# Seven half-block products in place of eight in the last product of a hybrid layer, and the recurrence's output in a score bank

## The chip, the cores and the metric

The kernel runs on one core of one Trainium2 chip. The metric is the device time of an execution in microseconds, the median of several runs. The engines are named as in the profile: PE is TensorE (PEld its weight loads), DVE is VectorE, ACT is ScalarE, POOL is GpSimd, SP is SyncE. Matmuls accumulate in PSUM, in eight banks of 128 x 512 float32; everything else lives in SBUF.

## The reference

One decoder layer on 512 tokens and 1024 channels. A combined input projection feeds a block-sparse attention branch (8 heads of 64) and a gated linear recurrence (4 heads of 128). Both branches are projected up to 1024 channels, gated and merged; then comes what this case is about:

```
h = x + merged @ w_out                                  # 1024 x 1024
ple = (p @ w_ple) * sigmoid(h @ w_ple_gate)             # 256 x 1024 and 1024 x 1024
out = h + ple
```

## The kernel before, in words

Activations lie with channels on the partitions and the 512 tokens along the free axis, so a block of 128 channels is one tile of 128 x 512. A float32 operand a is split into a high half (a copy on ACT in the reduced format fp32r, names ending in h) and a low half (the difference, on DVE, names ending in l). Each product of 128 x 128 weights is then three matmuls: high x high, low x high, high x low (`mm3`, L288).

After the branches come three stages, each over eight output blocks n of 128 channels:

- the merge (ua, L1032), which leaves mh and ml, eight blocks of each;
- the output product (h, L1042 to L1055): eight input blocks by three matmuls of 512 tokens, 24 in all, then `hf = h + x` on DVE (L1049) and its split into hh and hl;
- the last stage (L1067 to L1095): the small product pe of two input blocks (6 matmuls, p @ w_ple), the last product g of eight input blocks (24 matmuls, h @ w_ple_gate), the sigmoid on ACT (L1092), a multiplication by pe and an addition of hf on DVE (L1093, L1094), and the store. The last block is cut into two halves of 256 tokens, so that less is left to do after the last matmul.

Weight blocks of w_out and w_ple_gate (512 KB, tiles wf64 to wf79) are loaded by POOL's queue (L261) into four buffers, and split by `w_split` (L271 on ACT, L272 on DVE) two blocks ahead of use (LD, L41); loads run three further ahead (LATE, L43).

The order of PE's instructions is the order in which the code is written, with side work (attention, recurrence) let in by a clock of nominal times (`tick`, L130). A scheduler places the instructions of ACT, DVE, POOL and SP; `held` and `behind` pin one behind another, `high_priority` draws work forward. PSUM is given out from three pools: "mm" (3 banks, most products), "g" (2) and "a" (3, the attention's scores, and pe). A product that gets a bank waits until the last reader of what was in it is done.

The recurrence's output products (hop, L681 to L690) take a bank of "mm". At the program's start eight matmuls on constants (WARM, L47, L188) keep PE busy until the first operands are there.

## Time and profile before

| | us |
|---|---|
| median of 3 runs (458.33 to 459.59) | 458.77 |
| the profiled execution's own time | 456.21 |
| its span, first to last instruction | 454.4 |
| PE busy in the span | 448.5 |
| the output product h, from 352.39 | 43.52 |
| the last stage, 395.91 to the end | 58.5 |

The profile's durations are those of one execution, 2.6 us below the median; sums are made against its span. A row of the chain of waits in order of time has start, duration, engine, tile and line. A row of the groups has line, engine, operation, tiles and shapes, count, busy time, mean ns of one, and the idle time before it with what ended that. Matmul rows overlap: one lasts 0.389 us with 512 tokens, and the next starts 0.227 us later.

### The profile page before, as it was taken

How to read it: one execution, taken by the hardware profiler on the slowest of the kernel's cores; microseconds unless marked ns; L12 is line 12 of the kernel's file. 1: busy time of each engine (PE TensorE's matmuls, PEld its weight loads, DVE VectorE, ACT ScalarE, POOL GpSimd, SP SyncE). 2: the span in 40 equal slices, each digit the busy share in tenths (PEclk: the TensorE clock that was granted, in tenths of full speed). 3: DMA queues.
4: the chain of work that ended last, by engine and by line, in shares of the span. 5: the costliest groups of instructions: out<-in, count | busy, mean ns of one | idle time of the engine just before them, and what ended most of it. 6: DMA issues, size and time to landing. Idle time of an engine off the chain costs nothing.

```text
span 454.4 us, 8097 instructions
## 1 busy us (share of the span) xinstructions
PE 448.5 (99%) x3064; PEld 373.0 (82%) x3064; DVE 303.0 (67%) x616; ACT 275.4 (61%) x532; POOL 38.6 (8%) x77
## 2 busy tenths in 40 slices
PE   9999999999999999999999999999999999999996
PEld 8888888888888888878788888878888888888886
DVE  5869593886898787858995864654569744544322
ACT  5958574737689696879987894884335433222201
POOL 1000100000000000010101000101220100000000
PEclk9999999999999999999999999999999999999999
DMA  8802323167592446162526243365631644230111
GB/s 257 320 1 93 140 101 119 57 226 184 184 249 71 129 134 172 44 197 67 175 83 190 67 133 124 108 196 152 234 100 47 230 141 140 92 115 25 46 48 46
DMA packets 31846, 59.49 MB, mean 131 GB/s; under 512 B 6976, under 2 KB 16960, under 8 KB 31808
## 3 DMA queue, kind: packets, MB, share of 16 engines
q0 software_dynamic: 9056, 32.51, 21.5%
q1 hardware_dynamic: 22608, 26.47, 19.7%
q8 instruction: 24, 0.39, 0.4%
q14 instruction: 14, 0.11, 0.1%
q10 hardware_dynamic: 144, 0.01, 0.0%
HBM read 48.74 MB, written 4.98 MB: 118 GB/s over the span
## 4 chain that ended last, share of the span: by engine, by line
PE 86%; ACT 5%; DVE 4%; SPq 2%; DMA 1%; issue 1%; DVEq 0%
PE ga L288 10%; PE g L288 10%; PE h L288 10%; PE gb L288 5%; PE ub L288 5%; PE aq L418 5%; PE ak L418 5%; PE ua L288 5%; PE av L418 5%; PE bi L418 4%; PE bf L288 4%; PE bg L288 4%; PE ag L288 4%; PE pe L288 2%; PE bq L288 2%; SPq L859 2%
## 5 line engine op out<-in xcount | busy, mean ns | idle before, releaser
L271 ACT ACTIVATE wh<-wf 128x1024 fp32r<-128x1024 f32 (+1 forms) x78 | 75.5, 968 | 91.6 <-issue 32.2
L272 DVE TENSOR_TENSOR wl<-wf,wh 128x1024 fp32r<-128x1024 f32 (+1 forms) x78 | 86.5, 1109 | 49.5 <-ACT wh L271 49.2
L261 POOL DMA_DIRECT2D wf<-in_w_tr_dram x30 | 15.9, 530 | 171.6 <-DVE wl L272 133.7
L843 ACT ACTIVATE pb<-pb,ps 128x128 f32<-128x128 f32 (+3 forms) x32 | 17.7, 553 | 20.0 <-DVE ps L841 19.9
L288 PE MATMUL g<-hh,wh 128*128 128x512 f32 (+1 forms) x72 | 26.3, 365 | 0.0
L288 PE MATMUL g<-hl,wh 128*128 128x512 f32 (+1 forms) x72 | 26.3, 365 | 0.0
L288 PE MATMUL g<-hh,wl 128*128 128x512 f32 (+1 forms) x72 | 26.3, 365 | 0.0
L288 PE MATMUL gb<-xh,wh 128*128 128x512 f32 x64 | 25.1, 392 | 0.7 <-ACT hu L514 0.7
L288 PE MATMUL ga<-xh,wh 128*128 128x512 f32 x64 | 25.2, 394 | 0.0
L288 PE MATMUL gb<-xl,wh 128*128 128x512 f32 x64 | 24.9, 390 | 0.0
L288 PE MATMUL ga<-xh,wl 128*128 128x512 f32 x64 | 24.9, 389 | 0.0
L288 PE MATMUL ga<-xl,wh 128*128 128x512 f32 x64 | 24.9, 389 | 0.0
L288 PE MATMUL gb<-xh,wl 128*128 128x512 f32 x64 | 24.9, 389 | 0.0
L288 PE MATMUL h<-mh,wh 128*128 128x512 f32 x64 | 24.9, 389 | 0.0
L288 PE MATMUL h<-ml,wh 128*128 128x512 f32 x64 | 24.9, 389 | 0.0
L288 PE MATMUL h<-mh,wl 128*128 128x512 f32 x64 | 24.9, 389 | 0.0
L841 DVE CUSTOM_DVE_ANT_0 pb<-s,bias 128x128 f32<-128x128 f32 (+3 forms) x28 | 12.9, 491 | 6.6 <-DMA bias<-in_ed_dram 3.3
L1049 DVE TENSOR_TENSOR hf<-h,xres 128x512 f32<-128x512 f32 x8 | 5.5, 691 | 16.5 <-PE h L288 16.5
L845 ACT ACTIVATE pb<-pb,ps 128x128 f32<-128x128 f32 (+3 forms) x32 | 16.0, 550 | 0.0
L542 ACT ACTIVATE hx<-hx 128x512 f32<-128x512 f32 x24 | 14.8, 623 | 1.4 <-DVE hx L541 1.3
L288 PEld LDWEIGHTS g<-hh,wl 128*128 128x128 f32 x72 | 13.6, 189 | 2.2
L288 PEld LDWEIGHTS g<-hl,wh 128*128 128x128 f32 x72 | 13.6, 189 | 2.2
(346 smaller groups left out, 1244.8 us busy)
## 6 DMA issues: line engine op xcount, KB each, us to landing
wf<-in_w_tr_dram POOLq DMA_DIRECT2D x30, 512.0 KB, 3.8
wf<-in_w_tok_dram POOLq DMA_DIRECT2D x8, 512.0 KB, 3.5
wf<-in_w_up_dram POOLq DMA_DIRECT2D x16, 256.0 KB, 3.0
wf<-in_w_o_dram POOLq DMA_DIRECT2D x8, 512.0 KB, 4.6
wf<-in_w_g_dram POOLq DMA_DIRECT2D x8, 512.0 KB, 3.5
wf<-in_w_tok_dram SPq DMA_DIRECT2D x6, 512.0 KB, 6.9
pb<-pb SPq DMA_DIRECT2D x64, 48.0 KB, 2.7
bias<-in_ed_dram SPq DMA_DIRECT2D x8, 256.0 KB, 5.4
```

Source lines behind the costliest of these rows:

```text
L261: (G if len(wraw) >= FAR else nc.sync).dma_start(raw, ap)
L271: rounds[i] = A.activation(hi, wraw[i], AF.Copy)
L272: V.tensor_tensor(lo, wraw[i], hi.bitcast(F32), op=OP.subtract)
L288: dense.append(PE.matmul(ps, a[:, k, :], b[k], start=(n == 0), stop=(n == tot - 1)))
L418: dense.append(PE.matmul(banks[t], a[:, s_], b[:, kk, :], start=(k == 0 and i == 0), stop=(k == KD - 1 and i == 2)))
L542: A.activation(x, x, AF.Exp)
L841: in_order(V.tensor_tensor_reduce(p_, s_[:, so:so + nk], T[j][:, nk - 1::-1], -1.0, 3e38, OP.add, OP.min, st[:, 0:1]))
L843: A.activation(p_, p_, AF.Exp, bias=st[:, 0:1], scale=-1.0, accum_out=st[:, 1:2])
L845: A.activation(p_, p_, AF.Copy, scale=st[:, 2:3])
L859: nc.sync.dma_start(pt[32 * b:32 * b + 32, a], z[32 * a:32 * a + 32, b])
L1049: V.tensor_tensor(t, ps, xres, op=OP.add)
```

## The change

The last product is done by Strassen's method in Winograd's form. The output blocks are taken in pairs (p, p + 4), the eight input blocks in two halves of four (k and k + 4), the tokens in two halves of 256 (lh, rh). For a pair, weights a11, a12, a21, a22 (each four input blocks by 128 output channels) and h blocks b11, b12, b21, b22 give four output quarters by seven products instead of eight. A product is 4 input blocks x 3 matmuls of 256 tokens.

- On the weight side a pair needs s12 = (a21 + a22, that minus a11) and s34 = (a11 - a21, a12 minus the second of s12). The first of each is made on POOL, the second on DVE (`pairs_of_weights`). Then a11 with a12 (w1), s12 (w2), s34 (w3; two tiles w3 and w5 in pair 0) and a22 (w4) are split into high and low halves.
- On the h side `pairs_of_h` makes four differences of 256 tokens for each of the four k, on DVE, and splits seven halves of 256. Tiles: b (b11), bl (b21, b22), bt (products 5 and 6), bu (products 7 and 4; for k = 3 they share the tiles named bt3).
- Products 1 and 2 add up in one bank, 6, 7 and 4 in a second, 5 and 3 in a third. Between them ACT copies product 1 away (keep) and DVE keeps two sums, since later quarters need them. A quarter is then: an addition on DVE (not for the first), sigmoid on ACT, multiplication on DVE, addition of hf on POOL (on DVE in pair 3), and a store of 128 x 256. There are 16 stores instead of 9.
- The order of the output product becomes 0, 4, 1, 5, 2, 6, 3, 7 (PAIRED), and the weights come in the order of the pairs. The split of h blocks into hh and hl falls away. The preparation of pair 0's weights stands in the last three rounds of the output product, that of pair p + 1 in pair p.
- WARM is 9. The hop products take a bank of "a".

```diff
--- before.py
+++ after.py
@@ -44,7 +44,7 @@
 EARLY = (2, 3, 4, 5)
-WARM = 8
+WARM = 9
 WAIT = 16
...
+PAIRED = [n // 2 + 4 * (n % 2) for n in range(KD)]
 AHEAD = 150
@@ -243,10 +245,11 @@
         for n in range(KD):
             wseq.append((w_up[n, 0], 4, 128))
         late.append(len(wseq))
+        for n in PAIRED:
+            wseq.append((w_o[n], KD, 128))
+        late.append(len(wseq))
         for n in range(KD):
-            wseq.append((w_o[n], KD, 128))
-        for n in range(KD):
-            wseq.append((w_g[n], KD, 128))
+            wseq.append((w_g[n // 2 + 4 * (n % 2)], KD, 128))
     w_sequence()
@@ -262,7 +265,7 @@
             wraw.append(raw)
     def w_split(upto):
-        while len(wtile) <= min(upto, len(wseq) - 1):
+        while len(wtile) <= min(upto, late[1] - 1):
...
@@ -681,7 +684,7 @@
...
-            op_.append(bank("mm", f"hop{h}"))
+            op_.append(bank("a", f"hop{h}"))
...
@@ -1038,61 +1041,238 @@
...
-    hh, hl, hf = [], [], []
-    for n in range(KD):
-        ws = weight(w_o[n])
...
+    lh, rh = slice(0, 256), slice(256, 512)
+    hf, xt, wt, edge = {}, {}, {}, []
+    def pairs_of_weights(p):
+        r0, r1 = wraw[late[1] + 2 * p], wraw[late[1] + 2 * p + 1]
+        a11, a12, a21, a22 = [r[:, 4 * i:4 * i + 4] for r in (r0, r1) for i in range(2)]
+        s12 = pb[:, 6:8].rearrange("p a (k c) -> p a k c", k=4)
+        s34 = pb[:, 8:10].rearrange("p a (k c) -> p a k c", k=4)
+        def both(src, tag, name, shape, late_=False):
+            h_ = unit(tag[0], name + "h", R, shape)
+            l_ = unit(tag[1], name + "l", R, shape)
+            first = A.activation(h_, src, AF.Copy)
+            second = V.tensor_tensor(l_, src, h_.bitcast(F32), op=OP.subtract)
+            if late_:
+                held(first)
+                behind(first, edge[-2])
+                behind(second, edge[-1])
+            return h_, l_
+        w1 = both(r0, ("wh", "wl"), f"w1{p}", (128, KD, 128))
+        G.tensor_tensor(s12[:, 0], a21, a22, op=OP.add)
+        second = V.tensor_tensor(s12[:, 1], s12[:, 0], a11, op=OP.subtract)
+        if p:
+            behind(second, edge[-1])
+        wt[p] = {1: [t[:, 0:4] for t in w1], 2: [t[:, 4:8] for t in w1]}
+        yield
+        w2 = both(s12, ("wh", "wl"), f"w2{p}", (128, 2, 4, 128))
+        G.tensor_tensor(s34[:, 0], a11, a21, op=OP.subtract)
+        V.tensor_tensor(s34[:, 1], a12, s12[:, 1], op=OP.subtract)
+        wt[p].update({5: [t[:, 0] for t in w2], 6: [t[:, 1] for t in w2]})
+        yield
+        if p == 0:
+            wt[p][4] = both(a22, ("Q", "Q"), f"w4{p}", (128, 4, 128))
+            yield
+            wt[p][7] = both(s34[:, 0], ("SG", "SG"), f"w3{p}", (128, 4, 128))
+            yield
+            wt[p][3] = both(s34[:, 1], ("wh", "wl"), f"w5{p}", (128, 4, 128), True)
+            yield
+            return
+        w3 = both(s34, ("wh", "wl"), f"w3{p}", (128, 2, 4, 128))
+        wt[p].update({7: [t[:, 0] for t in w3], 3: [t[:, 1] for t in w3]})
+        yield
+        wt[p][4] = both(a22, ("YB", "YB"), f"w4{p}", (128, 4, 128))
+        yield
+    firsts = {}
+    def pairs_of_h(k):
+        ts = pb[:, 4:6].rearrange("p a (b c) -> p (a b) c", b=2)
+        b11, b12 = hf[k][:, lh], hf[k][:, rh]
+        if k % 2 == 0:
+            firsts[k // 2] = [unit("X", f"b{k}{i}", R) for i in "hl"]
+        first = [f[:, 256 * (k % 2):256 * (k % 2) + 256] for f in firsts[k // 2]]
...
+        xt[k] = {1: first, 2: [t[:, lh] for t in low], 3: [t[:, rh] for t in low],
+                 5: [t[:, lh] for t in t12], 6: [t[:, rh] for t in t12],
+                 7: [t[:, lh] for t in t34], 4: [t[:, rh] for t in t34]}
+        split(first[0], first[1], b11)
+        V.tensor_tensor(ts[:, 0], b12, b11, op=OP.subtract)
+        if k == 3:
+            split(xt[k][5][0], xt[k][5][1], ts[:, 0])
+        yield
+        b2 = hf[k + 4]
+        b21, b22 = b2[:, lh], b2[:, rh]
+        with tc.high_priority(offset=AHEAD if k == 3 else 0):
+            V.tensor_tensor(ts[:, 1], b22, ts[:, 0], op=OP.subtract)
+            if k == 3:
+                split(xt[k][6][0], xt[k][6][1], ts[:, 1])
+                split(low[0], low[1], b2)
+            V.tensor_tensor(ts[:, 3], b21, ts[:, 1], op=OP.subtract)
+            V.tensor_tensor(ts[:, 2], b22, b12, op=OP.subtract)
+            if k < 3:
+                split(t12[0], t12[1], pb[:, 4])
+                split(low[0], low[1], b2)
+            edge.append(A.activation(t34[0], pb[:, 5], AF.Copy))
+            edge.append(V.tensor_tensor(t34[1], pb[:, 5], t34[0].bitcast(F32), op=OP.subtract))
+        yield
...
+    def small_weights(n, late_=False):
+        if n // 2 not in small:
...
+            small[n // 2] = (pwh, pwl)
+    ph, pl = [], []
+    preps = {}
+    for i, n in enumerate(PAIRED):
+        ws = weight(w_o[n])
+        xres = unit("T", f"xres{n}")
+        nc.sync.dma_start(xres, xT[n])
+        if i == 5:
+            preps[0] = pairs_of_weights(0)
+            next(preps[0])
+        elif i == 6:
+            next(preps[0])
+            next(preps[0])
+            small_weights(0)
+        elif i == 7:
+            next(preps[0])
+            small_weights(4)
+        ps = bank("mm", f"h{n}")
+        mm3(ps, ws[0], ws[1], mh, ml, KD)
+        hf[n] = unit("H", f"hf{n}")
+        with tc.high_priority(offset=AHEAD if n == 7 else 0):
+            V.tensor_tensor(hf[n], ps, xres, op=OP.add)
+        if n < 4:
+            halves = pairs_of_h(n)
+        next(halves)
+        if i == 3:
+            for k in range(2):
+                nc.sync.dma_start(pb[:, 8 + k], pT[:, k])
+                h_ = unit("A", f"ph{k}", R)
+                l_ = unit("A", f"pl{k}", R)
+                split(h_, l_, pb[:, 8 + k])
+                ph.append(h_)
+                pl.append(l_)
+        if i >= 5:
+            w_load(late[1] + i - 3)
+    def merge(n, c, ps, pes, t, plus=None):
+        if plus is not None:
+            with tc.high_priority(offset=AHEAD):
+                V.tensor_tensor(t[:, c], ps, plus, op=OP.add)
+            ps = t[:, c]
+        A.activation(t[:, c], ps, AF.Sigmoid)
+        yield
+        V.tensor_tensor(t[:, c], t[:, c], pes()[:, c], op=OP.mult)
+        (V if n % 4 == 3 else G).tensor_tensor(t[:, c], t[:, c], hf[n][:, c], op=OP.add)
+        nc.sync.dma_start(out[n][:, c], t[:, c])
+    for p in range(4):
+        n0, n1 = p, p + 4
+        w_load(late[1] + 2 * p + 3)
+        tags = ("mm",) * 3 if p % 2 == 0 else ("a",) * 3
+        ba, bb, bc = [bank(t_, f"g{p}{i}")[:, lh] for i, t_ in enumerate(tags)]
+        dst = {1: ba, 2: ba, 6: bb, 7: bb, 4: bb, 5: bc, 3: bc}
+        pe0, pe1 = bank("g", f"pe{n0}"), bank("g", f"pe{n1}")
+        t0, t1 = unit("Q", f"sg{n0}"), unit("Q", f"sg{n1}")
+        keep = unit("KT", f"keep{p}")
+        keep2 = pb[:, 4 + p % 2, lh]
+        def product(i):
+            wh, wl = wt[p][i]
+            m = 0
+            for k in range(4):
+                bh, bl = xt[k][i]
+                for a, b in ((wh, bh), (wh, bl), (wl, bh)):
+                    dense.append(PE.matmul(dst[i], a[:, k], b, start=(m == 0 and i in (1, 6, 5)), stop=(m == 11),
+                              skip_group_check=i not in (1, 6, 5)))
+                    m += 1
+                tick(0.36)
+        whole = slice(0, 512)
+        if p == 0:
+            order = ["E0", 1, 5, 6, 2, 7, "E1", 4, 3]
+        elif p < 3:
+            order = [1, 6, 2, 5, 7, "E0", "E1", 4, 3]
+        else:
+            order = [1, 6, 5, 7, "E1", "E0r", 4, 3, 2, "E0l"]
+        ends = {}
+        for step in order:
+            if step == "E0":
+                ple(pe0, n0, whole)
+            elif step == "E1":
+                ple(pe1, n1, whole)
...
+            else:
+                product(step)
+            with tc.high_priority(offset=AHEAD):
+                if step == 1:
+                    kept = A.activation(keep[:, lh], ba, AF.Copy)
+                elif step == 6:
+                    edge.extend([kept, V.tensor_tensor(keep[:, rh], bb, keep[:, lh], op=OP.add)])
+                elif step == 7:
+                    V.tensor_tensor(keep2, bb, keep[:, lh], op=OP.add)
...
+            if p == 0 and step == 6:
+                next(preps[0])
+            if p == 1 and step in (5, 7):
+                small_weights(n0 + 1 if step == 5 else n1 + 1, True)
+            if p < 3 and step == 2:
+                preps[p + 1] = pairs_of_weights(p + 1)
+                next(preps[p + 1])
+            if p < 3 and step == "E1":
+                next(preps[p + 1])
+            if p < 3 and step == order[-1]:
+                next(preps[p + 1])
+                next(preps[p + 1])
```

What the change moves, at three places. In a name, the first number counts the tile and the second the buffer.

**PE, first round of the last product.** g0_0 is the product of output block 0; g00, g01 and g02 are the three banks of pair 0. Before:

```order
L288 MATMUL g0_0_4290<-hh0_3982,wh72_4183 128x512 [waits Activation_49]
L288 MATMUL g0_0_4290<-hl0_3983,wh72_4183 128x512
L288 MATMUL g0_0_4290<-hh0_3982,wl72_4184 128x512 [waits DVE_49]
L288 MATMUL g0_0_4290<-hh1_4021,wh72_4183 128x512
L288 MATMUL g0_0_4290<-hl1_4022,wh72_4183 128x512
L288 MATMUL g0_0_4290<-hh1_4021,wl72_4184 128x512
```

Now, from the end of product 1 through the start of product 5:

```order
L1214 MATMUL g00_4336<-b2l_4172,w10h_4190 128x256
L1214 MATMUL g00_4336<-b2h_4171,w10l_4191 128x256
L1214 MATMUL g00_4336<-b2h_4171,w10h_4190 128x256 [waits Activation_49]
L1214 MATMUL g00_4336<-b2l_4172,w10h_4190 128x256 [waits DVE_49]
L1214 MATMUL g00_4336<-b2h_4171,w10l_4191 128x256
L1214 MATMUL g02_4338<-bt0h_3987,w20h_4236 128x256
L1214 MATMUL g02_4338<-bt0l_3988,w20h_4236 128x256
L1214 MATMUL g02_4338<-bt0h_3987,w20l_4237 128x256
L1214 MATMUL g02_4338<-bt1h_4075,w20h_4236 128x256
L1214 MATMUL g02_4338<-bt1l_4076,w20h_4236 128x256
```

Each row has 256 tokens instead of 512. Before, an input block stood behind its own round; now the sums for product 5 must be there for four k after 12 matmuls of product 1. Up to the output product PE's order is the same as before.

**DVE, the last rounds of the output product**, from one residual sum hf to the next. Before (pwl are small weights, wl weights):

```order
L1049 TENSOR_TENSOR hf6_4214<-h6_4189,xres6_4187 128x512 [waits DMAHW3_49,PE_49]
L223 TENSOR_TENSOR pwl2_4365<-pb_70,pwh2_4364 128x512 [waits DVE_49]
L272 TENSOR_TENSOR wl73_4223<-wf73_4103,wh73_4222 128x1024 [waits DMASW7_49,Activation_49]
L223 TENSOR_TENSOR hl6_4217<-hf6_4214,hh6_4216 128x512 [waits Activation_49]
L1049 TENSOR_TENSOR hf7_4253<-h7_4228,xres7_4226 128x512 [waits DMAHW4_49,PE_49]
L223 TENSOR_TENSOR pwl4_4454<-pb_70,pwh4_4453 128x512 [waits DVE_49]
L272 TENSOR_TENSOR wl74_4280<-wf74_4142,wh74_4279 128x1024 [waits DMASW0_49,Activation_49]
```

Now (h blocks 3 and 7 come last; pb holds the sums, keep0 the kept sum):

```order
L1171 TENSOR_TENSOR hf3_4276<-h3_4251,xres3_4234 128x512 [waits DMAHW2_49,PE_49]
L1111 TENSOR_TENSOR pb_70<-hf3_4276 128x256 [waits DVE_49]
L1144 TENSOR_TENSOR pwl4_4297<-pb_70,pwh4_4296 128x512 [waits DMAHW3_49]
L1057 TENSOR_TENSOR w20l_4237<-pb_70,w20h_4236 128x1024 [waits Activation_49]
L1057 TENSOR_TENSOR w41l_4483<-wf75_4232,w41h_4482 128x512 [waits DMASW1_49,PE_49,Activation_49]
L225 TENSOR_TENSOR b2l_4172<-hf3_4276,b2h_4171 128x256 [waits Activation_49]
L225 TENSOR_TENSOR bt3l_4281<-pb_70,bt3h_4280 128x256 [waits Activation_49]
L1057 TENSOR_TENSOR w42l_4641<-wf77_4486,w42h_4640 128x512 [waits DMASW3_49,PE_49,Activation_49]
L1171 TENSOR_TENSOR hf7_4325<-h7_4300,xres7_4289 128x512 [waits DMAHW3_49,PE_49]
L1118 TENSOR_TENSOR pb_70<-hf7_4325,pb_70 128x256 [waits DVE_49]
L1123 TENSOR_TENSOR pb_70<-hf7_4325,hf3_4276 128x256
L1122 TENSOR_TENSOR pb_70<-hf7_4325,pb_70 128x256 [waits DVE_49]
```

Before, one low half of weights, one of h and one of small weights stood between two residual sums. Now seven steps stand there, three of them weights (w20l of pair 0, w41l and w42l of pairs 1 and 2), and six steps follow the last residual sum.

**ACT, the turn from pair 0 to pair 1.** Before, splits of weights and sigmoids alternated:

```order
L271 ACTIVATE wh76_4370<-wf76_4220 128x1024 [waits DMASW2_49,PE_49,Activation_49]
L1092 ACTIVATE sg1_0_4358<-g1_0_4333 128x512 [waits PE_49]
L271 ACTIVATE wh77_4411<-wf77_4277 128x1024 [waits DMASW3_49,DVE_49,PE_49]
L1092 ACTIVATE sg2_0_4406<-g2_0_4381 128x512 [waits PE_49]
L271 ACTIVATE wh78_4457<-wf78_4320 128x1024 [waits DMASW4_49,DVE_49,PE_49]
L1092 ACTIVATE sg3_0_4447<-g3_0_4422 128x512 [waits PE_49]
```

Now (w11, w21, w31 are weights of pair 1, w43 of pair 3; keep1 is the copy of product 1 of pair 1, from bank g10):

```order
L1056 ACTIVATE w11h_4408<-wf74_4182 128x1024 [waits DMASW0_49,PE_49,Activation_49]
L1191 ACT_TABLE_LOAD
L1191 ACTIVATE sg0_4341<-g00_4336 128x256 [waits PE_49]
L1056 ACTIVATE w21h_4438<-pb_70 128x1024 [waits DVE_49]
L1191 ACTIVATE sg4_4342<-sg4_4342 128x256 [waits DVE_49] x2
L1056 ACTIVATE w43h_4790<-wf79_4646 128x512 [waits DMASW5_49]
L1056 ACTIVATE w31h_4478<-pb_70 128x1024 [waits PE_49,Activation_49]
L1191 ACTIVATE sg0_4341<-sg0_4341 128x256 [waits DVE_49]
L1241 ACTIVATE keep1_4495<-g10_4488 128x256 [waits PE_49]
```

The copy keep1, on which the second product in that bank waits, stands behind w43h and w31h. w43h waits for the block wf79, which POOL loads behind these rows:

```order
L264 DMA wf77_4486<-in_w_g_dram 128x1024 [waits DVE_49]
L1065 TENSOR_TENSOR pb_70<-wf75_4232 128x512 [waits DVE_49]
L264 DMA wf78_4644<-in_w_g_dram 128x1024 [waits DVE_49,Pool_49]
L264 DMA wf79_4646<-in_w_g_dram 128x1024 [waits DVE_49,Activation_49]
L1194 TENSOR_TENSOR sg0_4341<-sg0_4341,hf0_3981 128x256 [waits DVE_49]
L1065 TENSOR_TENSOR pb_70<-wf77_4486 128x512 [waits DMASW3_49,DVE_49]
```

POOL's queue held loads alone at this place before; now sums stand between them, and the last load waits for DVE and ACT to be done with the buffer.

More of the change, by code (lines that the diff above doesn't have):

```diff
@@ L1056, in hybrid_layer_kernel @@
-    ph, pl = [], []
-    for k in range(2):
-        t = unit("A", f"pf{k}")
-        for i in range(2 - k):
-            w = 256 * (1 + k)
-            nc.sync.dma_start(t[:, w * i:w * i + w], pT[:, k, w * i:w * i + w])
-        h_ = unit("A", f"ph{k}", R)
-        l_ = unit("A", f"pl{k}", R)
-        split(h_, l_, t)
-        ph.append(h_)
-        pl.append(l_)
-    for n in range(KD):
-        if n % 2 == 0:
+    lh, rh = slice(0, 256), slice(256, 512)
+    hf, xt, wt, edge = {}, {}, {}, []
@@ L1069, in hybrid_layer_kernel, with ple @@
+    small = {}
+    def ple(bk, n, c):
+        pwh, pwl = small[n // 2]
+        mm3(bk[:, c], pwh[:, n % 2], pwl[:, n % 2], [a[:, c] for a in ph], [a[:, c] for a in pl], 2, 0.227 if c == slice(0, 512) else 0.12)
+    def small_weights(n, late_=False):
+        if n // 2 not in small:
             pw = pb[:, n // 2].rearrange("p (a b c) -> p a b c", a=2, b=2)
@@ L1072, in hybrid_layer_kernel @@
             pwl = unit("T", f"pwl{n}", R, (128, 2, 2, 128))
[L1073 to L1095 removed]
+            first = A.activation(pwh, pw, AF.Copy)
@@ new lines, in small_weights @@
+            second = V.tensor_tensor(pwl, pw, pwh.bitcast(F32), op=OP.subtract)
+            if late_:
+                held(first)
+                behind(first, edge[-2])
+                behind(second, edge[-1])
+            small[n // 2] = (pwh, pwl)
[33 more added lines that the diff above has]
+            w_load(late[1] + i - 3)
```

65 lines of the change are left out of this document (32 added, 33 removed).

## The prediction

> **What bounds the kernel now.** I read the page first, then the waits of TensorE, then the chain of waits in order of time, then the busy time of the last two stages.
>
> ```profile
> span 454.4 us, 8097 instructions
> PE 448.5 (99%) x3064; PEld 373.0 (82%) x3064; DVE 303.0 (67%) x616; ACT 275.4 (61%) x532; POOL 38.6 (8%) x77
> ```
> ```profile
> PE warm L189 <- PEq L1150: 0.8, 1, 0.8
> PE bf L288 <- DVE bg2s L486: 0.7, 1, 0.7
> PE gb L288 <- ACT hu L514: 0.7, 1, 0.7
> ```
> TensorE (PE) works 99% of the span. Its three waits come to 2.2 us, and one of them is the start. So time can only be won by giving PE less to do, and every new wait of PE is paid in full. The end of the chain of waits shows what the edited stage costs (start, duration, what; columns in us):
>
> ```profile
> 352.39 43.52 PE h L288 x192
> 395.91 1.36 PE pe L288 x6
> 397.27 5.44 PE g L288 x24
> ...
> 438.07 5.44 PE g L288 x24
> 443.51 0.71 PE pe L288 x6
> 444.22 5.76 PE g L288 x48
> 449.98 0.73 PE pe L288 x6
> ...
> 450.79 0.43 DVE sg L1093
> ...
> 451.25 0.42 DVE sg L1094
> ```
> The output product (h) runs 43.52 us without a gap, then come eight rounds of small product (pe) and last product (g), also without a gap. Seven rounds of g have 24 matmuls of 512 tokens in 5.44 us, 0.2267 us each. The eighth is cut into token halves: 48 matmuls of 256 tokens in 5.76 us, 0.12 us each. That row prices the new matmuls, and it shows that half a matmul costs more than half (0.1133). After the last matmul (449.98 + 0.73 = 450.71) two vector steps and the store fill 3.7 us to the end of the span.
>
> What stands beside PE in these stages (us of PE, weight loads, DVE, ACT and POOL, with counts; then clock, DMA share, GB/s):
>
> ```profile
> 352.39:395.91 43.52, 43.52 (x193) 36.04 (x193) 24.24 (x31) 14.44 (x20) 4.78 (x9) 1.00 0.46 154
> 395.91:450.54 54.63, 54.63 (x270) 46.40 (x269) 20.00 (x26) 12.53 (x17) 1.06 (x2) 1.00 0.16 58
> ```
> VectorE (DVE) is idle for 19 us of the first stage and 35 us of the second, ScalarE (ACT) for more, POOL nearly throughout. The clock is granted in full, so there is nothing to lose or win there.
>
> **The matmuls.** Before, g takes 7 x 5.44 + 5.76 = 43.84 us. Now each of four pairs of output blocks has seven products of 4 x 3 = 12 matmuls of 256 tokens: 4 x 84 x 0.12 = 40.32 us. The small products keep their 42 matmuls of 512 and 12 of 256. Term: **-3.52 us**. One eighth of 43.84 would be 5.48; the dearer half-width matmul eats the rest. Lower bound of this term: matmuls at 0.1133 would give 38.08, a saving of 5.76. The 48 matmuls of the row run at 0.12 throughout, with both operands changing as they will here, so I take 0.12.
>
> **The vector work around them**, priced by these groups (mean ns before the bar of idle time):
>
> ```profile
> L272 DVE TENSOR_TENSOR wl<-wf,wh 128x1024 fp32r<-128x1024 f32 x15 | 18.4, 1223 | 21.9 <-ACT wh L271 21.9
> L1049 DVE TENSOR_TENSOR hf<-h,xres 128x512 f32<-128x512 f32 x8 | 5.5, 691 | 16.5 <-PE h L288 16.5
> L1093 DVE TENSOR_TENSOR sg<-sg,pe 128x256 f32<-128x256 f32 x2 | 0.8, 422 | 4.3 <-PE pe L288 2.4 <-ACT sg L1092 2.0
> ```
> ```profile
> L271 ACT ACTIVATE wh<-wf 128x1024 fp32r<-128x1024 f32 x14 | 14.9, 1062 | 51.7 <-issue 32.2 <-PE g L288 15.7 <-PE h L288 2.2
> L222 ACT ACTIVATE hh<-hf 128x512 fp32r<-128x512 f32 x8 | 4.9, 613 | 0.0
> L1092 ACT ACT_TABLE_LOAD x1 | 1.3, 1283 | 0.0
> L1092 ACT ACTIVATE sg<-g 128x256 f32<-128x256 f32 x2 | 0.8, 384 | 5.5 <-PE g L288 5.5
> ```
> A pair takes PE 84 x 0.12 + 2 x 1.36 = 12.80 us. In that time DVE does three low halves of 1024 (3 x 1.22), one of 512 and two weight sums (3 x 0.69), and nine steps of 256 (two kept sums, three additions to products, four multiplications, 9 x 0.42): 9.5 us, and 10.9 where the second pair of small weights falls in. ACT does 3 x 1.06 + 0.61 + 5 x 0.38 = 5.7 us. Both fit under PE. Cost nothing while that cover holds; if DVE were over by some us, PE would pay them.
>
> The output product changes its order to 0, 4, 1, 5, ... so that the halves of h can be combined as they come. Two of its rounds (10.88 us) now carry, on DVE, two residual sums (2 x 0.69), five steps of 256 (2.1) and three low halves of 512 (2.07): 5.55 us. The weight blocks of w_g come on top, thickest in the last two rounds: by the order, two of 1024, two of 512, and small weights of 512, some 4.5 us; together about 10.1 of 10.88. It just fits.
>
> **The turn from h to g.** The last output block ends at 395.91. From there the part of h needed first is product 6's last quarter. Its chain: residual sum 0.69, one difference 0.42, high half on ACT 0.38, low half 0.42, which is 1.9 us, and 1.5 more when the two other differences and the 512-wide low half stand ahead on DVE: 3.4 us. PE has in front of it pe0 (1.36), products 1 and 5 (2 x 1.44) and three quarters of 6 (1.08): 5.3 us. So PE does not wait here, with 1.9 us to spare. What is late next if it fails: the residual sum stands on DVE behind the low halves w41l and w42l, and w42l waits for a weight block that POOL loads.
>
> **The turn from the first pair to the second.** Here I see a wait.
>
> ```profile
> wf<-in_w_o_dram POOLq DMA_DIRECT2D x8, 512.0 KB, 4.6
> ...
> wf<-in_w_g_dram POOLq DMA_DIRECT2D x8, 512.0 KB, 3.5
> ```
> The copy of product 1 of pair 1 (keep1), which frees its bank for product 2, stands on ACT behind w43h and w31h, and w43h needs the last weight block, whose buffer is free only when DVE has done pair 1's low half and sums. From the end of product 6 of pair 0 (395.91 + 1.36 + 3 x 1.44 = 401.6): kept sum 0.42, w50l 0.69, sum 0.69, w11l 1.22, sum 0.69 give 405.3; landing 3.5 us after the issue on POOL, 408.8; then 0.61 + 1.06 + 0.38 + 0.38 on ACT, 411.3, and some 0.5 for the issue itself (0.53 in the POOL row below). PE wants the bank at 395.91 + 12.80 + 2 x 1.44 = 411.6. So it waits 0.2 us, or 1.3 with the 4.6 us of the other row, and nothing if landings are quicker. I take **+0.5**, between them. The table load (1.28) falls into idle time of ACT just before. Later pairs load nothing.
>
> **The start.** Nine warming matmuls instead of eight:
>
> ```profile
> 0.78 3.75 PE L189 MATMUL warm<-const-float32-1.0 128*128 128x128 f32 x16 [0.78 <-PEq L1150]
> ...
> 4.11 0.29 DVE L369 CAST wh<-wf 128x256 fp32r<-128x256 f32 x1 [0.46 <-DMA wf<-in_w_tok_dram]
> ...
> 4.55 0.77 PE L449 MATMUL bi<-wh,gh 128*128 128x256 f32 x2
> ...
> 5.90 0.39 PE L449 MATMUL bi<-wh,gl 128*128 128x256 f32 x2
> ```
> The first real operand is ready at 4.40, and PE leaves the warming at 4.53: one more takes 3.75 / 8 = 0.47 us and is now ahead of the data. But the first six matmuls take 5.90 - 4.55 = 1.35 us (0.22 each) before the fast pace; those that move past that point run at 0.12. Six less two late ones at 0.12: **+0.2**, between 0 (data later than here) and 0.47.
>
> **The moved bank.** The wait of gb at 217.30 ends just after a vector step that reads bf's bank (216.47 + 0.69 = 217.16):
>
> ```profile
> 216.47 0.69 DVE L517 TENSOR_TENSOR hk<-ha,bf 128x512 f32<-128x512 f32 x1
> ...
> 217.07 1.22 DVE L272 TENSOR_TENSOR wl<-wf,wh 128x1024 fp32r<-128x1024 f32 x1
> ...
> 217.30 0.47 PE L288 MATMUL gb<-xh,wh 128*128 128x512 f32 x1 [0.71 <-ACT hu L514]
> ```
> In the changed program this gb gets a bank that bf held last, as before, and bf the one that bg2 held, as before. The recurrence's products go into a score bank whose last reader is long done. PE's order is the same up to the output product. Term **0**; between -1.4, if both waits went, and +0.7, if one more of the same size came.
>
> **The sum** against the profiled execution: -3.52 + 0.5 + 0.2 = -2.8, so a span of 451.6 instead of 454.4, and 456.21 - 2.8 = 453.4 for that execution. The median shown is 458.77, 2.6 above it; I take the change off the median: **456.0 us**.
>
> **Rival 1, slower: POOL's additions stop DVE.** Eight sums of weights (512) and twelve last additions (256) move to POOL, which adds nothing in this trace. Its nearest rows:
>
> ```profile
> L261 POOL DMA_DIRECT2D wf<-in_w_g_dram x8 | 4.2, 530 | 40.6 <-DVE wl L272 40.6
> L197 POOL MEMSET sc<- 128x512 f32 x1 | 0.5, 530 | 0.0
> masks.py:199 POOL TENSOR_SCALAR_AFFINE_SELECT ident<-ident 128x128 f32<-128x128 f32 x1 | 0.3, 285 | 0.0
> ```
> A 512-wide sum costs between 0.53 (the fill) and 4 x 0.285 = 1.14 us (the row that also reads); I take 1.1, it reads two. If DVE stood still for each, a pair would cost DVE 9.5 + 2 x 1.14 + 4 x 0.57 = 14.1 us against PE's 12.80: 1.3 late in each of the three pairs with POOL work, and 1.4 more for the small weights, 5.3 in all: 458.77 - 3.52 + 0.2 + 5.3 = **460.8**. It decides from (12.80 - 9.5) / 4 = 0.82 us a sum. Against it: neighbouring DVE rows overlap by about 0.09 us (216.47 + 0.69 against a next start at 217.07), 18 of them 1.6 us, which brings 14.1 to 12.5, and DVE has idle places that POOL's steps may take. For it: nothing measured. The Trainium skill, page "SBUF — State Buffer", section "Who interferes with whom", says exactly this of a vector instruction with two SBUF inputs and a GpSimd instruction that reads SBUF: the second to issue blocks until the first is done. By that rule alone the time would be the 460.8 above; no row here can test it, as POOL's loads only issue. Because of it I give this rival more than a small chance.
>
> **Rival 2: the preparation is late in several places.** The landing of 4.6 costs 1.3 at the second pair, and the thin cover of the last two output rounds (10.1 of 10.88, one POOL sum of 1.14 beside it) brings the residual sum late by more than the 1.9 us to spare, say 0.7: 458.77 - 3.52 + 0.2 + 2.0 = **457.5**. For it: everything for pair 0 stands in one DVE queue. Against: each sum was taken with full durations.
>
> **Rival 3: no wait at all, and the two old waits go** with the moved bank: 458.77 - 3.52 - 1.4 = **453.9**. Against: the banks just named.
>
> **Chances.** The forecast 0.60 (own range 455.2 to 457.0), rival 1 0.12, rival 2 0.20, rival 3 0.08. Range 454.8 to 458.9: it takes in the forecast, rival 2 and part of both ends. A measurement of this kernel can tell 0.3%, 1.4 us, so faster means below 457.4: forecast, rival 3 and a part of rival 2, 0.74. Within 0.3%: 0.16; slower: 0.10.
>
> **What would show it.** The g products at 0.12 us each and 40.3 us in all (else the first term is wrong); a PE wait at the second product on pair 1's bank, 0 to 1.3 us; no PE wait after pe0; POOL additions of about 1.1 us, with DVE steps beside them at 0.69 and 1.22 as before (rival 1: DVE gaps or stretched steps that end with POOL's); the first product at about 5.0; gb's and bf's waits still there. The forecast is wrong if PE's waits in the last stage exceed 2 us or if the weight preparation, not PE, sets a pair's 12.80 us.

## The result, and the profile after

The changed kernel took 456.44 us (median of 5 runs, 455.12 to 456.55) against 458.33 for the kernel before on the same chip; the ratio, estimated from all runs and not from these two medians (whose quotient is 0.9959), is 0.9947, 95% interval 0.9922 to 0.9973. Forecast were 456.0 us and a ratio of 456.0 / 458.77 = 0.994. The changed kernel is faster by about half a per cent.

The two profiles seem to say otherwise. First line and engines of the page, changed kernel:

```profile
span 454.7 us, 8514 instructions
PE 446.2 (98%) x3186; PEld 376.3 (83%) x3186; DVE 334.8 (74%) x680; ACT 289.1 (64%) x561; POOL 60.3 (13%) x97
```

The span is 0.3 us longer than the 454.4 of before, though PE is busy 2.3 us less. The waits of PE (waiting tile, what it waited for, us in total, times, longest) show where that went:

```profile
PE ag L291 <- DVE ps L844: 1.5, 1, 1.5
PE warm L191 <- PEq L1330: 0.8, 1, 0.8
PE bf L291 <- DVE bg2s L489: 0.7, 1, 0.7
PE gb L291 <- ACT hu L517: 0.7, 1, 0.7
PE ga L291 <- issue: 0.6, 1, 0.6
```

ag, bf, gb and ga are tiles of products that run far ahead of the last stage, so none of these waits lies in it. Two are new, ag at 186 us and ga at 284; for ga the profile names nothing that it waited for. The end of the chain of waits in order of time (start, duration, what):

```profile
355.33 43.52 PE h L291 x192
398.85 1.36 PE pe L291 x6
400.21 7.19 PE g L1214 x60
407.40 1.39 PE pe L291 x6
408.79 10.35 PE g L1214 x84
...
445.44 4.32 PE g L1214 x36
449.76 0.73 PE pe3l L291 x6
...
450.59 0.43 DVE sg L1193
...
451.04 0.42 DVE sg L1194
```

The output product begins at 355.33 instead of 352.39, 2.94 us late. From there to the last matmul it is 450.49 - 355.33 = 95.16 us; before it was 450.71 - 352.39 = 98.32. The edited stage alone is 3.16 us shorter. Behind the last matmul 4.21 us follow instead of 3.69. So three stretches have to be told apart: the front up to the output product, the stage, and the end.

### The profile page after: what moved, and what is told of

The parts are those of the page before. It is cut to its first block, busy times and chain, and to the rows that moved or that the text cites. A ratio compares the mean times of both kernels' runs of the same rounds, so it can differ in the third digit from the quotient of the medians.

```text
span 454.7 us, 8514 instructions
## 1 busy us (share of the span) xinstructions
PE 446.2 (98%) x3186; PEld 376.3 (83%) x3186; DVE 334.8 (74%) x680; ACT 289.1 (64%) x561; POOL 60.3 (13%) x97
## 4 chain that ended last, share of the span: by engine, by line
PE 86%; ACT 5%; DVE 3%; SPq 2%; DMA 1%; issue 1%; DVEq 0%
PE ga L291 10%; PE h L291 10%; PE g L1214 9%; PE gb L291 5%; PE ub L291 5%; PE aq L421 5%; PE ak L421 5%; PE ua L291 5%; PE av L421 5%; PE bi L421 4%; PE bf L291 4%; PE bg L291 4%; PE ag L291 4%; PE bq L291 2%; SPq L862 2%; PE pe L291 2%
## 5 line engine op out<-in xcount | busy, mean ns | idle before, releaser
L274 ACT ACTIVATE wh<-wf 128x1024 fp32r<-128x1024 f32 (+1 forms) x70 | 67.0, 958 | 56.7 <-PE ub L291 13.5
L275 DVE TENSOR_TENSOR wl<-wf,wh 128x1024 fp32r<-128x1024 f32 (+1 forms) x70 | 76.7, 1096 | 27.5 <-ACT wh L274 27.2
L1191 ACT ACTIVATE sg<-sg 128x256 f32<-128x256 f32 x12 | 5.0, 414 | 20.3 <-DVE sg L1189 20.3
L264 POOL DMA_DIRECT2D wf<-in_w_up_dram x16 | 8.6, 538 | 57.2 <-DVE wl L275 46.8
L851 DVE STREAM_TRANSPOSE pb<-pb 128x512 f32<-128x512 f32 x20 | 13.7, 697 | 3.1 <-ACT pb L848 1.9
L291 PEld LDWEIGHTS gb<-xh,wh 128*128 128x128 f32 x64 | 12.0, 188 | 3.9 <-ACT hu L517 1.5
L264 POOL DMA_DIRECT2D wf<-in_w_tok_dram x8 | 4.4, 550 | 80.3 <-ACT avv L481 45.9
L291 PEld LDWEIGHTS ga<-xh,wl 128*128 128x128 f32 x64 | 12.0, 188 | 3.5 <-issue 1.0
```

Source lines behind the costliest of these rows:

```text
L264: (G if len(wraw) >= FAR else nc.sync).dma_start(raw, ap)
L274: rounds[i] = A.activation(hi, wraw[i], AF.Copy)
L275: V.tensor_tensor(lo, wraw[i], hi.bitcast(F32), op=OP.subtract)
L291: dense.append(PE.matmul(ps, a[:, k, :], b[k], start=(n == 0), stop=(n == tot - 1)))
L851: V.transpose(z[:, :, b_, :].rearrange("p b (n c) -> p b n c", c=32), pb[:, b_].rearrange("p (n b c) -> p b n c", b=4, c=32))
```

## The experiments

All kernels below were read by these three stretches, from rows like those just shown. Front: from the first gate product bf, some 49 us after the start, to the output product. Stage: to the last matmul. End: to the end of the span, which is given to 0.1 us. The last columns are PE's waits at ag and at gb (where DVE hk is named); the first experiment shows what lies behind them. No ratio stands where a kernel ran only once, for its profile; of these runs only the stretches are read.

| kernel | bf at | front | stage | end | ag | gb | ratio to before |
|---|---|---|---|---|---|---|---|
| before, as shown | 48.94 | 303.45 | 98.32 | 3.69 | 0 | 0 | 1 |
| before, again | 49.42 | 306.56 | 98.32 | 3.70 | 1.5 | 1.0 | |
| changed | 49.26 | 306.07 | 95.16 | 4.21 | 1.5 | 0 | 0.9947 |
| changed, again | 48.50 | 306.27 | 95.15 | 4.18 | 1.1 | 1.1 | 0.9946 |
| late loads of p | 49.03 | 306.53 | 95.17 | 4.17 | 0.6 | 1.3 | 0.9947 |
| the same, 8 warming matmuls | 48.47 | 306.39 | 95.16 | 4.18 | 1.1 | 1.2 | 0.9937 |
| late loads, recurrence in "mm" | 49.25 | 307.45 | 95.15 | 4.15 | 1.2 | 1.2 | 0.9945 |
| eight products of half blocks | 49.06 | 306.20 | 100.69 | 3.75 | 1.2 | 1.3 | |
| all sums on DVE | 49.50 | 306.76 | 95.42 | 3.82 | 1.4 | 0.9 | |
| POOL's weight sums twice | 48.96 | 308.13 | 100.92 | 3.89 | 1.9 | 1.2 | |
| p in pieces | 48.59 | 305.97 | 95.17 | 3.97 | 1.2 | 1.2 | 0.9948 |
| one sum behind the kept sum | 48.65 | 306.16 | 95.58 | 4.21 | 1.0 | 1.3 | |
| early biases | 49.34 | 302.85 | 95.16 | 4.15 | 0 | 0 | 0.987 |
| before with early biases | 48.82 | 304.22 | 98.32 | 3.74 | 0 | 1.3 | 0.995 |

Where the order of the stage's instructions is the same, the stage repeats within 0.02 us; the front does not.

**The kernel before, profiled again.** No edit.

> The kernel before, unchanged, profiled a second time. In the first profile its output product began at 352.39 us and the span was 454.4. Theory 1 (what comes ahead of the output product repeats): 352.4 again within 0.3, span 454.4. Theory 2 (the exchanges by DMA in the attention land at other times in each execution): the output product begins up to 3 us later, with a PE wait of 1 us or more that the first profile doesn't show; then the 2.9 us by which the changed kernel's profile is late at that point (355.33) is in part no work of the change.

It took 459.84 us. Chain and waits of this execution:

```profile
355.98 43.52 PE h L288 x192
...
453.57 0.73 PE pe L288 x6
```
```profile
PE ag L288 <- DVE ps L841: 1.5, 1, 1.5
PE gb L288 <- DVE hk L517: 1.0, 1, 1.0
```

Theory 2 holds. The front took 306.56 us, not 303.45, with two waits that the first profile lacks. Both go back to landings. DVE waits for an exchange ahead of a transposition (pb), and hk stands behind it on DVE; and DVE waits for the bias ahead of the softmax. An exchange is a group of 16 DMAs that move blocks of the attention weights from one part of pb to another (the expectations call them mask exchanges). In the first profile that transposition waited for nothing; here it does, and the bias is late too:

```profile
161.74 0.70 DVE L848 STREAM_TRANSPOSE pb<-pb 128x512 f32<-128x512 f32 x1
```
```profile
164.79 0.71 DVE L848 STREAM_TRANSPOSE pb<-pb 128x512 f32<-128x512 f32 x1 [2.19 <-DMA pb<-pb]
184.39 0.29 DVE L841 CUSTOM_DVE_ANT_0 pb<-s,bias 128x128 f32<-128x128 f32 x1 [3.16 <-DMA bias<-in_ed_dram]
```

All profiles together bear this out. DVE waited at this transposition for nothing in the first profile, 0.97 us with early biases and 1.16 in the changed kernel, and in these three gb did not wait for hk. It waited 2.2 to 2.6 us in the other eleven, and there gb waited 0.9 to 1.3.

The profile that the prediction rests on was a lucky one: its own time of 456.21 lies below all 17 timings of before beside this run (457.6 to 460.18, median 459.15), and of all 67 timings of that kernel on record one is lower (455.63). With fronts of 306.4 on both sides the spans would be 49 + 306.4 + 98.32 + 3.7 = 457.4 and 49 + 306.4 + 95.16 + 4.2 = 454.8; with the 1.8 us that lie around each span, 459.2 and 456.6. The medians are 458.3 to 459.2 in five sets of timings of before, and 456.44 and 456.45 in two of the changed kernel.

**The load of p, late.** In the changed kernel one of two loads of p stands on SP between two groups of 16 exchanges (162.69 us); before, all of them came after 350 us.

```diff
+    gate = dense[-50]
-    nc.sync.dma_start(pb[:, 8 + k], pT[:, k])
+    behind(nc.sync.dma_start(pb[:, 8 + k], pT[:, k]), gate)
```

> The changed kernel, only that both loads of p stand on SP's queue behind the mask exchanges of the attention, as in the kernel before (in the changed kernel one of them stands at 162.69 us, between the two groups of 16 exchanges). The order of PE, DVE, ACT and POOL is untouched. Theory 1 (this load delays the last exchange, for which DVE waits 1.16 us there): DVE's wait at the transposition goes, the bias is issued 1.3 us earlier, PE's wait of 1.5 us before the product ag goes; span 453.2 instead of 454.7, median 455.1, ratio 0.992. Theory 2 (executions differ by themselves): the wait comes in some executions as before, the timed ones again lie at two levels 1.3 us apart, median 456.4, ratio 0.995.

Theory 1 falls. DVE still waits for the exchange, and longer (changed kernel first, then this one):

```profile
163.43 0.71 DVE L851 STREAM_TRANSPOSE pb<-pb 128x512 f32<-128x512 f32 x1 [1.16 <-DMA pb<-pb]
```
```profile
164.66 0.71 DVE L851 STREAM_TRANSPOSE pb<-pb 128x512 f32<-128x512 f32 x1 [2.56 <-DMA pb<-pb]
```

The ratio is 0.9947 (0.9927 to 0.9966), that of the changed kernel. The load costs nothing that could be measured; the exchange is late without it too.

**Eight warming matmuls**, with the late loads.

```diff
-WARM = 9
+WARM = 8
```

> As the last kernel, with eight warming matmuls instead of nine. Theory 1 (my term of the sum): the first product starts at 4.5 instead of 4.96, and the stretch to 6.8 us is 0.35 shorter, so everything is 0.35 earlier: span 452.9, median 454.8. Theory 2 (what is ahead of the bound by other waits swallows it): the first product is earlier, the last matmul is not, and the median is that of the last kernel within 0.2.

Ratio 0.9937 (0.9916 to 0.9959), median 0.6 us lower than with nine (456.2 and 456.79): the direction of theory 1, inside the intervals. The first product starts at 4.18 us instead of 4.61. Over all profiles bf begins at 48.91 on average with eight (8 profiles, 48.47 to 49.42) and 49.08 with nine (6, 48.50 to 49.50). That is 0.17 us where 0.2 was predicted, but single profiles of either kind spread over a whole us, so neither its size nor its sign is settled.

**The recurrence's products back in their old bank**, with the late loads.

```diff
-            op_.append(bank("a", f"hop{h}"))
+            op_.append(bank("mm", f"hop{h}"))
```

> As the kernel with the late loads of p, but the recurrence's output products again take one of the three banks of most products; no engine's order changes. Theory 1 (my term of 0): PE's waits before bf and gb stay at 0.7 each, the span is that of the kernel with the late loads within 0.3. Theory 2 (the bank matters): the product that follows in the recurrence's bank waits for its last reader; PE has one more wait of 0.7 to 1.4 us in front of ag, bq or bg, and the span is longer by that.

Theory 1 by the waits and by the ratio: bf and gb wait 0.7 each as before, the ratio is 0.9945 (0.9926 to 0.9964). The profiled span is not within 0.3 us, it is 1.1 longer. Of the front's 0.9, 0.6 come with the wait for the bias (1.2 instead of 0.6); no wait for a bank is new.

**Eight products of half blocks**, in the kernel before.

```diff
-        parts = 1 if n < KD - 1 else 2
+        parts = 2
...
-            def ple():
+            def ple(s_=s_ if n == KD - 1 else slice(0, 512)):
...
-            if last:
+            if last and n == KD - 1:
```

The second and third change keep the small product whole in seven blocks.

> The kernel before, its last product in eight products of half blocks throughout: every output block in two token halves of 256 as the last one was, with the small product still whole for seven blocks, 16 stores of 128 x 256. Read between the start of the output product and the last matmul (98.32 us before, 95.16 changed) and from the last matmul to the end of the span (3.70 before, 4.17 changed). Theory 1 (a matmul of 256 costs 0.12, more than half of 0.2267): 98.32 + 7 x 0.32 = 100.56. Theory 2 (the dear half-width is the last block's alone, where it waits for nothing else): under 99.0. For the end, theory A (what counts is on which of SP's eight completion semaphores the last store is counted, since the end waits for them in turn; two come after it before, four in the changed kernel, three here): 3.93. Theory B (16 stores): 4.17.

The stage took 100.69 us, 2.37 longer than before: theory 1 (2.24). So the half-width matmul is dear everywhere: each of the seven blocks took 5.75 us instead of 5.44, and the whole small product behind it 1.39 instead of 1.36. Against eight products in its own width the method saves 100.69 - 95.16 = 5.5 us, nearly the eighth of 8 x 5.76 us, and 2.4 of it go to the width. The end was 3.75 us with 16 stores: theory B falls, and A's 3.93 isn't met either.

**All sums on DVE**, with the late loads.

```diff
-        G.tensor_tensor(s12[:, 0], a21, a22, op=OP.add)
+        V.tensor_tensor(s12[:, 0], a21, a22, op=OP.add)
-        G.tensor_tensor(s34[:, 0], a11, a21, op=OP.subtract)
+        V.tensor_tensor(s34[:, 0], a11, a21, op=OP.subtract)
-        (V if n % 4 == 3 else G).tensor_tensor(t[:, c], t[:, c], hf[n][:, c], op=OP.add)
+        V.tensor_tensor(t[:, c], t[:, c], hf[n][:, c], op=OP.add)
```

> As the kernel with the late loads of p, with the eight sums of weights and the twelve last additions on DVE instead of POOL. Read between the start of the output product and the last matmul (95.16). Theory 1 (POOL's additions relieve DVE): DVE gets 8 x 0.69 + 12 x 0.42 = 10.6 us more and loses the stretching (some 6.6 us); in the pair with the small weights it is over PE's 12.80 by about 0.7, so 95.9 to 97. Theory 2 (POOL's additions cost DVE as much as they take from it, by making it stand still): 95.16 within 0.3, or shorter.

95.42 us, 0.26 longer: theory 2 by its number, in one run. Its reason, that POOL's sums cost DVE as much as they take from it, holds by somewhat more than half, as the groups show. What POOL's work does to DVE is seen when the groups of the two kernels are laid side by side (mean ns before the last bar). Changed kernel, POOL and DVE:

```profile
L1194 POOL TENSOR_TENSOR sg<-sg,hf 128x256 f32<-128x256 f32 x12 | 10.2, 861 | 9.6 <-DVE sg L1193 9.5
L1072 POOL TENSOR_TENSOR pb<-wf,wf 128x512 f32<-128x512 f32 x4 | 6.2, 1545 | 7.8 <-DMA wf<-in_w_g_dram 4.6 <-DVE w31l L1057 1.9 <-DVE w32l L1057 1.3
L1065 POOL TENSOR_TENSOR pb<-wf 128x512 f32<-128x512 f32 x4 | 5.6, 1388 | 11.0 <-DVE w20l L1057 4.2 <-DVE w22l L1057 3.8 <-DMA wf<-in_w_g_dram 2.9
```
```profile
L1144 DVE TENSOR_TENSOR pwl<-pb,pwh 128x512 fp32r<-128x512 f32 x4 | 4.2, 1062 | 0.0
L1066 DVE TENSOR_TENSOR pb<-pb,wf 128x512 f32<-128x512 f32 x4 | 3.6, 899 | 0.0
L1118 DVE TENSOR_TENSOR pb<-hf,pb 128x256 f32<-128x256 f32 x4 | 3.1, 776 | 0.1
L1123 DVE TENSOR_TENSOR pb<-hf,hf 128x256 f32<-128x256 f32 x4 | 2.8, 692 | 0.0
L225 DVE TENSOR_TENSOR b2l<-hf,b2h 128x256 fp32r<-128x256 f32 x2 | 1.9, 962 | 0.0
L1193 DVE TENSOR_TENSOR sg<-sg,pe 128x256 f32<-128x256 f32 x15 | 6.2, 417 | 3.3 <-ACT sg L1191 1.8 <-PE pe L291 1.5
```

The same DVE steps with POOL free of sums:

```profile
L1144 DVE TENSOR_TENSOR pwl<-pb,pwh 128x512 fp32r<-128x512 f32 x4 | 2.8, 690 | 0.0
L1066 DVE TENSOR_TENSOR pb<-pb,wf 128x512 f32<-128x512 f32 x4 | 2.7, 687 | 0.0
L1118 DVE TENSOR_TENSOR pb<-hf,pb 128x256 f32<-128x256 f32 x4 | 1.7, 424 | 0.1
L1123 DVE TENSOR_TENSOR pb<-hf,hf 128x256 f32<-128x256 f32 x4 | 1.7, 421 | 0.0
L225 DVE TENSOR_TENSOR b2l<-hf,b2h 128x256 fp32r<-128x256 f32 x2 | 0.8, 422 | 0.0
```

Single steps show how it happens. A sum on POOL runs from 378.99 to 380.46; a DVE step issued at 379.23 ends only after it:

```profile
378.99 1.47 POOL L1072 TENSOR_TENSOR pb<-wf,wf 128x512 f32<-128x512 f32 x1
```
```profile
379.23 1.52 DVE L1123 TENSOR_TENSOR pb<-hf,hf 128x256 f32<-128x256 f32 x1
```

The five groups shown first lose 4 x (0.37 + 0.21 + 0.35 + 0.27) + 2 x 0.54 = 5.9 us of DVE, and two smaller ones (L1073, w43l) 0.6 more, beside 22.0 us of POOL. The sums cost DVE 10.6 us if it does them itself. Giving them to POOL relieves it by some 4, under half of that.

It also goes the other way. Where the DVE step began first, POOL's sum is the one that took longer, and the step kept its 0.68:

```profile
388.43 0.68 DVE L1144 TENSOR_TENSOR pwl<-pb,pwh 128x512 fp32r<-128x512 f32 x1
```
```profile
388.48 2.12 POOL L1072 TENSOR_TENSOR pb<-wf,wf 128x512 f32<-128x512 f32 x1 [4.57 <-DMA wf<-in_w_g_dram]
```

With the late loads the same sum began behind these DVE steps, at 389.74, and took 1.28.

**POOL's weight sums twice**, with the late loads: each of the eight is written a second time with the same numbers.

```diff
-        G.tensor_tensor(s12[:, 0], a21, a22, op=OP.add)
+        for _ in range(2):
+            G.tensor_tensor(s12[:, 0], a21, a22, op=OP.add)
...
-        G.tensor_tensor(s34[:, 0], a11, a21, op=OP.subtract)
+        for _ in range(2):
+            G.tensor_tensor(s34[:, 0], a11, a21, op=OP.subtract)
```

> As the kernel with the late loads of p, with each of the eight sums of weights on POOL done twice (the second writes the same numbers again). Theory 1 (my first rival's mechanism is real: DVE stands still while POOL adds, and was hidden only by DVE's room): DVE's steps beside POOL stretch by another 0.6 to 1.3 us for each, DVE goes over PE's 12.80 us in the pairs 0 to 2, and start of the output product to last matmul grows from 95.16 by 2 to 5 us. Theory 2 (POOL only shares, DVE has room for more): under 0.5 longer.

100.92 us, 5.76 longer, a little beyond theory 1's 2 to 5. PE now waits for DVE in the stage:

```profile
PE g L1217 <- DVE b2l L225: 1.5, 1, 1.5
PE g L1217 <- DVE pb L1248: 1.4, 2, 1.2
...
PE g L1217 <- DVE hf L1174: 0.7, 1, 0.7
PE g L1217 <- DVE bt3l L225: 0.6, 1, 0.6
```

Eight more sums of 1.4 us (11 us of POOL) cost PE half of their length. The mechanism of the first rival is real. How much of the loss is DVE's stretching is not separated: the doubled sums also hold up two of POOL's loads, which now wait for them (at 387.33 and 406.01 us).

**p in pieces**: the late loads of p in three pieces each, with eight warming matmuls.

```diff
-                behind(nc.sync.dma_start(pb[:, 8 + k], pT[:, k]), gate)
+                for c0, c1 in ((0, 176), (176, 352), (352, 512)):
+                    behind(nc.sync.dma_start(pb[:, 8 + k, c0:c1], pT[:, k, c0:c1]), gate)
```

> As the kernel with the late loads of p and eight warming matmuls, with each of the two loads of p in three pieces: four more DMAs of SP, so that the last store is counted on the last of the eight completion semaphores that the end waits for in turn. From the last matmul to the end of the span, theory A (each semaphore that still has to be waited for behind that of the last store costs 0.24 us, from 3.70 with two and 4.17 with four): 3.2 to 3.3, median 0.9 under that of the kernel with eight warming matmuls (456.2), ratio 0.992. Theory B (number of stores, length of the program): 4.17, ratio 0.9937.

The end took 3.97 us, neither 3.2 nor 4.17, and the ratio is 0.9948 (0.9922 to 0.9974). Both theories fall. What goes with the end in all fourteen profiles is how many transfers of kind "instruction" on queue 14 follow within 3 us behind the span: none where it is 3.69 to 3.75 (before, twice; eight half products; before with early biases), one where it is 3.82 to 3.97 (all sums on DVE, POOL's sums twice, p in pieces), two where it is 4.15 to 4.21 (the rest). That is no proof, since they come after the last instruction that the profile shows. The end's 0.5 us stay unexplained.

**One sum behind the kept sum**, with late loads and eight warming matmuls. In the changed kernel PE hesitates in pair 0 at product 4 (w40h), where 0.23 us instead of 0.12 pass to the next matmul, and starts it 0.08 late; DVE does the kept sum (L1245) that frees the bank just then:

```profile
408.71 0.39 PE L1214 MATMUL g<-bu0h,w40h 128*128 128x256 f32 x1
408.94 0.28 PE L1214 MATMUL g<-bu0l,w40h 128*128 128x256 f32 x1
```
```profile
407.91 0.41 DVE L1193 TENSOR_TENSOR sg<-sg,pe 128x256 f32<-128x256 f32 x1
408.24 0.42 DVE L1245 TENSOR_TENSOR pb<-g,keep 128x256 f32<-128x256 f32 x1
```

The sum of weights (L1073) stands at 407.31, ahead of both.

```diff
-        V.tensor_tensor(s34[:, 1], a12, s12[:, 1], op=OP.subtract)
+        fourth = V.tensor_tensor(s34[:, 1], a12, s12[:, 1], op=OP.subtract)
+        if p == 1:
+            behind(fourth, summed[0])
...
-                    V.tensor_tensor(keep2, bb, keep[:, lh], op=OP.add)
+                    summed.append(V.tensor_tensor(keep2, bb, keep[:, lh], op=OP.add))
```

> As the kernel with the late loads of p and eight warming matmuls, with one sum of weights of pair 1 put behind the kept sum after product 7 of pair 0 on DVE. Theory 1 (PE's 0.26 to 0.36 us of waiting in pair 0 is for this kept sum, behind which the bank of product 4 comes free, and for the addition after it): the wait at the first matmul of product 4 goes, start of the output product to last matmul 94.85 to 95.0. Theory 2 (the wait is the change from 512 to 256 tokens, in the matmuls themselves): 95.16.

The hesitation at product 4 went, so it was DVE's order: theory 1 for the wait, not for the time. The stage became 95.58, not 94.85 to 95.0: PE now waits some 0.6 us one product later, for the addition that frees the third bank:

```profile
410.18 0.36 PE L1218 MATMUL g<-bl0h,w50h 128*128 128x256 f32 x1 [0.49 <-DVE sg L1193]
```

Moving this one step moved the wait and made it longer.

**The biases early**, with late loads and eight warming matmuls, to test the front's waits: the next head pair's two biases are issued ahead of the second group of exchanges.

```diff
-                if i == 0:
-                    for j in range(2):
...
+                if n == 0:
+                    biases(0)
...
+                if i == NS - 1 and hp + 1 < HPAIRS:
+                    biases(hp + 1)
                 pts[n] = sorted_groups(i, z)
```

> As the kernel with the late loads of p and eight warming matmuls, with the two biases of the next head pair issued on SP ahead of the second group of 16 mask exchanges instead of behind it. Theory 1 (the front's wait of 1.1 to 1.5 us before ag is for the bias, issued last of 34): this wait goes, the median falls by 1.1 to 1.5 to some 455, ratio 0.991; the exchanges are 1.1 us later, which the attention's output products have room for. Theory 2 (the exchanges are the chain): they are late by 1.1 us plus the transfer of 512 KB, PE waits as long at another place, ratio 0.9937 or higher.

Theory 1, and more: 453.19 us, ratio 0.987 (0.9848 to 0.9893), beside 456.45 for the changed kernel on the same chip (0.9946, 0.9926 to 0.9966). Of PE's waits the one at ag is gone, and in this execution, where DVE waited only 0.97 us for the exchange, the one at gb too:

```profile
PE gb L291 <- ACT hu L517: 0.7, 1, 0.7
PE av L421 <- ACT wh L379: 0.6, 1, 0.6
PE bf L291 <- DVE bg1s L489: 0.3, 1, 0.3
```

This version beats both kernels. The changed kernel without any edit, run beside it:

> The changed kernel once more, on the chip of the two kernels below. By the accounts so far (start of the output product to last matmul 95.16 instead of 98.32 us, end 4.17 instead of 3.70, start 0.2 later) it is 2.5 us faster than the kernel before where the front is the same: ratio 0.9945. If the first measurement's 0.9947 was partly the front's luck, the ratio lies outside 0.993 to 0.996.

It took 456.45 us, ratio 0.9946, inside the range named. So the first ratio was not one front's luck.

**Early biases in the kernel before**, the same edit.

> The kernel before, with only the biases of the next head pair issued on SP ahead of the second group of mask exchanges. Theory 1 (the front's gain is independent of the last product): the ratio is that of the changed kernel with early biases without the change's part, 0.987 / 0.9945 = 0.9925; start of the output product to last matmul 98.32 us, end 3.7. Theory 2 (the early biases help only with the changed bank of the recurrence's products): ratio 0.997 or higher.

Ratio 0.995 (0.9932 to 0.9968), weaker than the 0.9925 of theory 1 but clear of 1. The wait at ag went here too, the one for the exchange (1.3 us) stayed. The version with all edits is worth 0.987 (0.9848 to 0.9893). It also has the late loads of p and eight warming matmuls, which with the change gave 0.9937; times 0.995 that is 0.989, inside the interval. That the parts do more together than apart is not shown.

## Why the prediction was right, and where not

**The bound.** "PE works 99% of the span, so time can only be won by giving PE less to do" was read from one execution. All others but the two with early biases have a front 2.5 to 4.7 us longer, and moving three pairs of DMAs won about as much as the change did (0.995 beside 0.9946), with PE's matmuls left as they were. The sum held all the same, because it was taken off the median, and the stage does not depend on the front.

**The matmuls, -3.52: right.** 60 of them take 7.19 us, 0.12 each, and the eight half products confirmed the price from the other side.

**The turn from h to g: right.** No wait after pe0.

**The turn from pair 0 to pair 1, +0.5: wrong place.** ACT, at the turn:

```profile
412.04 0.63 ACT L1056 ACTIVATE w43h<-wf 128x512 fp32r<-128x512 f32 x1 [0.71 <-DMA wf<-in_w_g_dram]
412.58 1.04 ACT L1056 ACTIVATE w31h<-pb 128x1024 fp32r<-128x1024 f32 x1
413.53 0.40 ACT L1191 ACTIVATE sg<-sg 128x256 f32<-128x256 f32 x1
413.83 0.37 ACT L1241 ACTIVATE keep<-g 128x256 f32<-128x256 f32 x1
```

The copy is done at 414.20; PE writes that bank next at 414.66. The chain was as described, w43h waits for its load, but 0.46 us are to spare. The step that failed is the "some 0.5 for the issue itself": the load was issued at 408.55 and w43h began at 412.04, 3.5 us with the issue in them, so it was counted twice; and four ACT steps follow each other 0.3 us faster than their durations add up. In its place the stage lost 0.36 us elsewhere, which the prediction had given no room of its own: 0.27 at products 4 and 3 of pair 0 (84 matmuls in 10.35 us instead of 10.08), of which DVE's late kept sum is shown for product 4, and some 0.1 in small products beside half-width ones (1.39 instead of 1.36).

**DVE's cover** was judged too wide. The stretch of pair 1 in the changed kernel (us of PE, weight loads, DVE, ACT and POOL, with counts; clock, DMA share, GB/s):

```profile
411.60:424.40 12.80, 12.80 (x98) 12.31 (x98) 11.91 (x17) 6.18 (x11) 6.03 (x8) 1.00 0.13 41
```

DVE is busy 11.9 of 12.80 us, where the working said 10.9 with the small weights; the stretched steps are in the difference. PE waited for nothing in the pairs 1 to 3, so what was left of the cover was enough.

**Rival 1** named the right mechanism and the wrong share. It let DVE stand still for the whole of each sum and put the point of decision at 0.82 us a sum. The sums took 1.39 and 1.55 us on average, beyond that point, and PE still lost at most 0.27. The runs show DVE held up only where a step with both operands in SBUF began during a sum; where the step came first, POOL waited. The argument against it counted 18 overlapping DVE rows; its own list has 15, which makes 12.7 and not 12.5.

**The start, +0.2, is not settled; the moved bank, 0, is right** as far as the waits tell. The first product started at 4.63 us, not at about 5.0: the profile before was late here (4.55), five of the eight with eight warming matmuls start it at 4.18 to 4.21.

**Missing: the end.** The 3.7 us behind the last matmul were carried over unchanged. They became 4.2, for a reason that stays open. The load of p on SP was missing too, but cost nothing that could be measured.

The sum as measured: -3.16 in the stage (-3.52 and +0.36) and +0.5 at the end, with the unsettled +0.2 at the start: -2.5, which fits the ratios 0.9946 and 0.9947 (2.4 to 2.5 us). The forecast of -2.8 came near it partly by luck: the +0.5 for a turn where nothing was lost stood in for 0.36 us at another place, and for part of an end that was not in the sum.

## What to carry to other kernels

A stage that repeats within 0.02 us can be read from one profile; a span cannot, when DMA landings decide elsewhere. Before building on a profile, compare its own time with the median: if it lies at their lower edge, waits may be missing from it that most executions have. And work that is handed to POOL is in part paid for on DVE where DVE's steps with both operands in SBUF run beside it.
